# Attention with pairs of heads on the two halves of the matmul array, results feature-major

## The chip, the cores and the metric

One core of one Trainium2 chip. The time is device microseconds of one execution; a kernel's time is the median of its runs, and lower is better. PE is the matmul engine, PEld its weight loads, DVE the vector engine, ACT the scalar engine, POOL the general engine, SP the engine that issues most DMAs.

## The reference

256 tokens with 1024 features pass through two stacked blocks of two layers each, all in float32. The attention of the first block has 8 heads of 64 features in three dilation groups, whose results are mixed by a softmax over their log-sum-exps; the kernel takes that as one softmax over the keys of all three groups. The second block has 8 query heads on 2 key heads, with a learned sink in the denominator, beside a Fourier mix; both halves are normed and projected.

```
# first block, per layer
x = x + 0.5 * swiglu_ffn(rmsnorm(x, ffn1_norm), ffn1_w_up, ffn1_w_down)
q, k, v, glu_in, gates = split(rmsnorm(x, mix_norm) @ w_in + b_in)
q, k = apply_rope(rmsnorm(q, q_norm)), apply_rope(rmsnorm(k, k_norm))
for g, (window, dil) in enumerate(((128, 1), (512, 4), (2048, 16))):
    o, l = dilated_window_attn(q[:, :, g], k[:, :, g], v[:, :, g], dil, window // (2 * dil))
y_attn = sum(softmax(lses)[..., None] * outs) @ w_attn_proj
y_conv = conv_module(glu_in, ...)
x = x + (sigmoid(g_attn) * y_attn + sigmoid(g_conv) * y_conv) @ w_out
x = rmsnorm(x + 0.5 * swiglu_ffn(rmsnorm(x, ffn2_norm), ...), final_norm)

# second block, per layer
u, q, k, v = split(rmsnorm(x, norm1) @ w_in)
y_f = real(fft2(u, norm="ortho")) @ w_f + b_f
s = where(|qpos - kpos| <= 128, (q . k) / 8, -inf)      # 4 query heads share one key head
y_a = softmax(concat(s, sink))[..., :-1] @ v
x = x + concat(rmsnorm(y_f, g_fourier_out), rmsnorm(y_a, g_attn_out)) @ w_o
x = x + (silu(conv3(h @ w_gate)) * conv3(h @ w_val)) @ w_down    # h = rmsnorm(x, norm2)
```

## The kernel before, in words

The residual stream lives on chip with features on partitions: eight tiles of [128 features, 256 tokens]. Every weight passes through on-chip memory once, in units of at most [128, 1024], in the order of use. `unit` (L317) hands out the next one; `ahead` (L304) splits it into a rounded part on ACT (L312) and the rest on DVE (L313), three units ahead, and `fetch` (L294) loads six ahead on SP's queue. A float32 product of weights is three passes of a faster float32r format on such split operands: `mm3` (L326 to L332). Products in the attention are plain float32, which PE runs as two instructions each.

The program is written in one order; a scheduler in the compiler then orders each engine's instructions by that priority and by when it reckons them ready, so that neighbouring pieces can interleave. Two pools hold the accumulators, four banks each of [128, 512]: `acc` (for products of weights) and `aux` (scores, transposes, sums).

First block, `mixer` (L620). q and k are normed, rotated and transposed to features on partitions, two heads to a tile of 128 rows (64 rows each); v stays with tokens on partitions. Attention goes over 16 steps a layer, (tile of 128 queries, head), in a pipeline of three (L816 to L839): `scores` (L765) of step i, one product of 256 keys and two of 128 keys on the 64 rows of the head; `soft` (L774), mask and maximum on DVE (L777), exp with its sum on ACT (L779); `pv_transpose` (L886) of step i-1, four transposes (L889) of the unnormalised probabilities and a copy (L891); `pv` (L782) of step i-2, four products with the transposed probabilities standing and 64 columns of v streaming (L785), result with tokens on partitions. Half units of the gates' products (`gate`, L806, 24 instructions) stand between the steps. `finish` (L789), once per tile of queries, divides by the sums (L793) and transposes the result to features on partitions (L797) for the projection. The mean and variance of the conv branch (`norm_mean`, `norm_cols`, `norm_rows`) run at steps 2, 5 and 7.

Second block, `mixer2` (L899). Eight steps a layer (L1108 to L1122), each for two heads of one parity, which lie on the same 64 rows: `soft` (L1064) with two scores of 256 keys (L1069), mask (L1074), exp (L1080); then transposes and `pv` (L1084, products L1088). The Fourier products (`f1`, `f2`, `f3`) and the first half of the projection (`proj(0, .)`) fill in by the table `fill` (L1046). `finish` (L1090) divides, takes the mean square of the result over its features on ACT and scales by its inverse root; `attn_operand` (L1123) transposes the result (L1127) and splits it. `proj(1, ob)` (L1024) adds the attention half to x.

The two edges of a half-array product in the code of before:

```
pr, ro = h // 2, slice((h % 2) * HD, (h % 2) * HD + HD)
nc.tensor.matmul(s[:, :256], qT[0][ro, pr, ts], kT[0][ro, pr, :], start=True, stop=True)
nc.tensor.matmul(Y[t][:, h * HD:(h + 1) * HD], pT[:, i * P:(i + 1) * P], w, start=i == 0, stop=i == 3)
```

Of the kernel before, what the change touches and what calls it, by code (L numbers as in the profile page):

```python
"""Two stacked transformer blocks (dilated-attention conformer, then a Fourier / windowed-GQA block),
256 tokens, 1024 features, two layers each, on one core.

The residual stream lives on chip feature-major: eight tiles [128 features, 256 tokens].
Every weight passes through SBUF once, in the order of its use.  Each float32 product is three
float32r passes on operands that are split on chip into a rounded part and the rest:
W x = Wl xh + Wh xl + Wh xh.
In the first block the tokens are ordered by (t mod 4, t div 4), so that the dilated groups are
blocks on the diagonal of a tile of 128 queries.
"""  # L10
# [45 lines left out]
FIRST = {1: -5, 3: -4, 5: -3, 7: -2}  # L56
# buffers of the weight stream, and how many units its splits and its loads run ahead
# [70 lines left out]
def shape_tables():  # L128
# [29 lines left out]
    # cosines at the frequencies 0..128, sines at 1..127: the rest follows by symmetry  # L158
# [35 lines left out]
# ----------------------------------------------------------------------------------------------  # L194
class Kernel:
# [130 lines left out]
    def mm3(self, out, wh, wl, xh, xl, start, stop, skip=False):  # L326
        """out += W^T x, stationary W"""
# [6 lines left out]
    def split(self, src, hi, lo, scale=None):  # L334
        """hi = rounded src * scale, lo = the rest"""
# [10 lines left out]
    def behind(self):  # L346
        """The block's work on ScalarE and VectorE queues up behind the last split."""
# [4 lines left out]
    def square_sum(self, blocks, scales=None):  # L352
        """Sum over blocks of (block * scale)^2, elementwise on [128, 256]"""
# [951 lines left out]
```

## Time and profile before

| | |
|---|---|
| median of 3 runs | 2011.82 us (1998.09, 2011.82, 2012.04) |
| profiled execution, its span | 1994.0 us |
| PE busy | 1972.2 us, 99% |
| DVE busy | 1393.5 us, 70% |
| ACT busy | 1121.9 us, 56% |
| attention stages, first block | 374 to 456 and 1066 to 1150 us |
| attention stages, second block | 1454 to 1504 and 1736 to 1787 us |

The profiled execution's own time beside its span is not recorded apart from the three runs; the fastest of them, 1998.09 us, is 4.1 us above its span. Times in the profile count from the first instruction. Durations of PE's instructions include their way through the array and overlap; the distance between two starts is what one costs in a stream.

### The profile page before, as it was taken

What the parts mean: (1) busy time and instruction counts of PE and PEld (TensorE: products, weight loads), DVE (VectorE), ACT (ScalarE), POOL (GpSimd) and SP (SyncE); (2) the same over time, 40 slices, a digit from 0 to 9 for tenths busy, and PEclk for the clock granted to TensorE, in tenths of its full rate; (3) what the DMA queues carried; (4) which work ended last, traced back from release to release, by engine and by line L of the source; (5) the groups of instructions that cost most, each with busy time, mean ns of one, the idle gap of its engine ahead of it and who ended that gap; (6) DMA issues with size and microseconds to landing.
All of it is one profiled execution on the core that took longest, in us unless ns stands there. A gap on an engine that the chain in (4) does not pass through costs nothing. (4 is left out here: it accounts for less than half of the span.)

```text
span 1994.0 us, 37071 instructions
## 1 busy us (share of the span) xinstructions
PE 1972.2 (99%) x14760; PEld 1881.0 (94%) x14760; DVE 1393.5 (70%) x2364; ACT 1121.9 (56%) x2133; POOL 113.9 (6%) x111
## 2 busy tenths in 40 slices
PE   8999999999999999999999999999999999999999
PEld 8999878899999999998788999999889999899999
DVE  6765687857666576656877567666768985669973
ACT  5544555647544455445556575444676764577662
POOL 1000022100000000000212000000100000100000
PEclk9999999999999999999999999999999999999999
DMA  8655655434555555556545245556334655524654
GB/s 263 194 179 182 218 169 167 154 96 159 180 182 183 176 177 191 175 185 212 177 165 165 79 154 180 183 178 182 122 127 149 199 177 179 181 96 161 203 179 125
DMA packets 97260, 339.09 MB, mean 170 GB/s; under 512 B 11430, under 2 KB 13574, under 8 KB 96960
## 3 DMA queue, kind: packets, MB, share of 16 engines
q1 hardware_dynamic: 93024, 326.63, 50.5%
q0 software_dynamic: 2944, 8.11, 1.7%
q8 instruction: 115, 1.88, 0.4%
q10 hardware_dynamic: 1120, 2.00, 0.3%
q14 instruction: 57, 0.47, 0.1%
HBM read 335.65 MB, written 1.05 MB: 169 GB/s over the span
## 5 line engine op out<-in xcount | busy, mean ns | idle before, releaser
L313 DVE TENSOR_TENSOR wl<-raw,wh 128x1024 fp32r<-128x1024 f32 (+1 forms) x634 | 758.7, 1199 | 351.2 <-ACT wh L312 346.2
L312 ACT ACTIVATE wh<-raw 128x1024 fp32r<-128x1024 f32 (+1 forms) x634 | 655.3, 1037 | 582.8 <-PE acc L332 273.1
L330 PE MATMUL acc<-xh,wl 128*128 128x256 f32 x1760 | 502.8, 286 | 4.6 <-DVE wl L313 4.5
L331 PE MATMUL acc<-xh,wh 128*128 128x256 f32 x1760 | 499.7, 284 | 0.0
L332 PE MATMUL acc<-xl,wh 128*128 128x256 f32 x1760 | 498.5, 283 | 0.0
L330 PEld LDWEIGHTS acc<-xh,wl 128*128 128x128 f32 x1760 | 338.1, 192 | 6.3 <-DVE wl L313 5.3
L331 PEld LDWEIGHTS acc<-xh,wh 128*128 128x128 f32 x1760 | 338.2, 192 | 0.8
L332 PEld LDWEIGHTS acc<-xl,wh 128*128 128x128 f32 x1760 | 338.0, 192 | 0.0
L330 PE MATMUL acc<-hh,wl 128*128 128x256 f32 x1056 | 298.8, 283 | 0.0
L331 PE MATMUL acc<-hh,wh 128*128 128x256 f32 x1056 | 298.8, 283 | 0.0
L332 PE MATMUL acc<-hl,wh 128*128 128x256 f32 x1056 | 298.8, 283 | 0.0
L330 PEld LDWEIGHTS acc<-hh,wl 128*128 128x128 f32 x1056 | 202.8, 192 | 0.0
L331 PEld LDWEIGHTS acc<-hh,wh 128*128 128x128 f32 x1056 | 202.8, 192 | 0.0
L332 PEld LDWEIGHTS acc<-hl,wh 128*128 128x128 f32 x1056 | 202.8, 192 | 0.0
L578 PE MATMUL acc<-wl,xh 128*128 128x512 f32 x480 | 189.7, 395 | 0.5 <-DVE wl L313 0.5
L579 PE MATMUL acc<-wh,xh 128*128 128x512 f32 x480 | 187.9, 392 | 0.0
L580 PE MATMUL acc<-wh,xl 128*128 128x512 f32 x480 | 187.8, 392 | 0.0
L330 PE MATMUL acc<-xn,wl 128*128 128x256 f32 x608 | 172.1, 283 | 0.0
L331 PE MATMUL acc<-xn,wh 128*128 128x256 f32 x608 | 172.1, 283 | 0.0
L332 PE MATMUL acc<-xn,wh 128*128 128x256 f32 x608 | 172.1, 283 | 0.0
L330 PEld LDWEIGHTS acc<-xn,wl 128*128 128x128 f32 x608 | 116.7, 192 | 0.0
L331 PEld LDWEIGHTS acc<-xn,wh 128*128 128x128 f32 x608 | 116.7, 192 | 0.0
(278 smaller groups left out, 3072.3 us busy)
## 6 DMA issues: line engine op xcount, KB each, us to landing
raw<-wts SPq DMA_DIRECT2D x576, 512.0 KB, 3.4
raw<-wts SPq DMA_DIRECT2D x48, 384.0 KB, 3.1
brow<-b_in POOLq DMA_DIRECT2D x26, 256.0 KB, 3.8
raw<-dft SPq DMA_DIRECT2D x4, 512.0 KB, 3.5
tab<-tab ACTq DMA_DIRECT2D x1, 1024.0 KB, 8.1
out<-x SPq DMA_DIRECT2D x8, 128.0 KB, 3.5
raw<-dft SPq DMA_DIRECT2D x2, 384.0 KB, 3.4
wraw<-conv_w POOLq DMA_DIRECT2D x6, 124.0 KB, 4.9
```

What stands on the lines that cost most here:

```text
L312: nc.scalar.activation(h[:, :n], r[:, :n], AF.Copy)
L313: nc.vector.tensor_tensor(lo[:, :n], r[:, :n], h[:, :n].bitcast(F32), op=ALU.subtract)
L330: mm(out, wl, xh, start=start, stop=False, **k)
L331: mm(out, wh, xh, start=False, stop=False, **k)
L332: mm(out, wh, xl, start=False, stop=stop, **k)
L578: mm(accs[t], xh[k][:, ts], wl[:, c], start=k == 0, stop=False)
L579: mm(accs[t], xh[k][:, ts], wh[:, c], start=False, stop=False)
L580: mm(accs[t], xl[k][:, ts], wh[:, c], start=False, stop=k == KB - 1)
```

## The change

In both blocks a step takes two heads whose features lie on the two halves of the 128 rows. First block: 8 steps a layer, (pair of heads, tile of queries); the scores of the two heads alternate, each into its own `aux` bank. The probabilities are divided by their sum before the transposes. In `pv`, 64 columns of v stand and the transposed probabilities stream; the two heads' results go to the lower and upper 64 partitions of one bank, so the result has features on partitions, and `finish` only splits it. The results take two `acc` banks from the start of the attention. One or two half gates stand in each of ten iterations. Second block: 4 steps a layer, (key head, tile of queries), each with four heads, two on each half; `fill` is regrouped to six iterations of three pieces. The inverse root of the attention output's mean square is taken by a sum over partitions and applied to the product of `proj(1, .)`. Comments and docstrings are removed throughout, with the line numbers kept; those hunks are left out, and of removed lines (they stand above) only the first of a run.

```diff
@@ -758,47 +758,50 @@
             if j + 2 < len(QKV):
                 rows.append(bias_row(QKV[j + 2][0] * AW + QKV[j + 2][1] * 512))
         self.exp_table()
-        Y = [None, None]
...
+        half = lambda h: slice(h * HD, (h + 1) * HD)
+        Y = [self.acc("Y") for _ in range(2)]
+        def scores(t, j):
+            s = [self.aux("s") for _ in range(2)]
             ts = slice(t * P, (t + 1) * P)
-            nc.tensor.matmul(s[:, :256], qT[0][ro, pr, ts], kT[0][ro, pr, :], start=True, stop=True)
...
+            for g in range(3):
+                c, ks = (slice(0, 256), slice(0, 256)) if g == 0 else (slice(128 + g * P, 256 + g * P), ts)
+                for h in range(2):
+                    nc.tensor.matmul(s[h][:, c], qT[g][half(h), j, ts], kT[g][half(h), j, ks], start=True, stop=True)
             return s
-        def soft(t, h, s, rden):
...
+        def soft(t, s):
+            e = [self.t2("e") for _ in range(2)]
+            m, rden = self.small("m", 2), self.small("rden", 2)
+            for h in range(2):
+                nc.vector.tensor_tensor_reduce(e[h], s[h], self.m1[t], scale=1.0, scalar=-3e38, op0=ALU.add, op1=ALU.max,
+                                               accum_out=m[:, h:h + 1])
             nc.vector.tensor_scalar_mul(m, m, -1.0)
-            stat["exp"] = nc.scalar.activation(e, e, AF.Exp, bias=m, scale=1.0, accum_out=rden[:, h:h + 1])
+            for h in range(2):
+                stat["exp"] = nc.scalar.activation(e[h], e[h], AF.Exp, bias=m[:, h:h + 1], scale=1.0,
+                                                   accum_out=rden[:, h:h + 1])
+            nc.vector.reciprocal(rden, rden)
+            for h in range(2):
+                nc.vector.tensor_scalar_mul(e[h], e[h], rden[:, h:h + 1])
             return e
-        def pv(t, h, pT):
...
+        def pv(t, j, pT):
+            ks = [(0, 0), (0, 1), (1, t), (2, t)]
+            out = Y[j // 2][:, j % 2 * S + t * P:j % 2 * S + (t + 1) * P]
+            for i, (g, tt) in enumerate(ks):
+                for h in range(2):
+                    c = tt * 512 + (j * 2 + h) * HD
+                    nc.tensor.matmul(out[half(h)], vv[g].rearrange("p a b -> p (a b)")[:, c:c + HD], pT[h][:, i * P:(i + 1) * P],
+                                     start=i == 0, stop=i == 3)
         yT = [self.t4("yTh", F32R), self.t4("yTl", F32R)]
-        def finish(t, den):
...
+        def finish(i):
+            self.split(Y[i].rearrange("p (j c) -> p j c", j=2), *[y[:, i * 2:i * 2 + 2] for y in yT])
         blk = lambda tiles, b: tiles[b // 4][:, b % 4]
         ga, gc = [self.t4("ga"), self.t4("ga")], [self.t4("gc"), self.t4("gc")]
@@ -812,32 +815,30 @@
                 nc.vector.tensor_tensor(blk(ga, n), a[:, :256], R, op=ALU.mult)
                 nc.vector.tensor_tensor(blk(gc, n), a[:, 256:], R, op=ALU.mult)
-        steps = [(t, h) for t in range(2) for h in range(NH)]
...
+        steps = [(j, t) for j in range(NH // 2) for t in range(2)]
+        later = {1: norm_mean, 3: norm_cols, 4: norm_rows}
+        gates = [(n, hf) for n in range(KB) for hf in range(2)]
         soft1, tr1 = None, None
         for i in range(len(steps) + 2):
             soft0 = tr0 = None
             if i < len(steps):
-                t, h = steps[i]
-                soft0 = (t, h, soft(t, h, scores(t, h), den[t]))
+                j, t = steps[i]
+                soft0 = (j, t, soft(t, scores(t, j)))
+            gate(*gates.pop(0))
             if soft1 is not None:
-                tr0 = (soft1[0], soft1[1], self.pv_transpose(soft1[2]))
-            if i % 4 != 3:
+                tr0 = (*soft1[:2], [self.pv_transpose(e) for e in soft1[2]])
+            if i % 2 == 0:
                 gate(*gates.pop(0))
             if tr1 is not None:
-                t, h, pT = tr1
...
+                j, t, pT = tr1
+                pv(t, j, pT)
+                if j % 2 and t:
+                    finish(j // 2)
             if i in later:
                 later[i]()
             soft1, tr1 = soft0, tr0
         def sigmoids(g, o_):
             with self.tc.issue_after(stat["silu"].ins):
                 for i in range(KB):
@@ -1032,7 +1033,9 @@
                 kk = half * 4 + k
                 self.mm3(out, wh[:, c], wl[:, c], oph[kk], opl[kk], k == 0 and ob % 2 == 0, k == 3, skip=True)
             if half == 1:
-                nc.vector.tensor_tensor(x[ob], x[ob], out, op=ALU.add)
+                t = self.t1("as")
+                nc.vector.tensor_tensor(t, out, cell["Ra"], op=ALU.mult)
+                nc.vector.tensor_tensor(x[ob], x[ob], t, op=ALU.add)
         def fourier_sum(ob):
             t = self.t1("fs")
@@ -1043,95 +1046,90 @@
         def later(name, f):
             return lambda: cell.update({name: f()})
-        fill = {0: [lambda: f1(0)], 1: [lambda: f1(1)], 2: [lambda: f2(0)], 3: [lambda: f2(1)],
...
+        fill = {0: [lambda: f1(0)], 1: [lambda: f1(1), lambda: f2(0)], 2: [lambda: f2(1), lambda: (f3(0), f3(1))],
+                3: [lambda: (f3(2), f3(3)), later("s", lambda: self.square_sum([yf[:, b] for b in range(4)]))],
+                4: [lambda: proj(0, 0), lambda: proj(0, 1), later("c", lambda: self.rms_cols(cell["s"], 512))],
+                5: [lambda: proj(0, 2), lambda: proj(0, 3), later("R", lambda: self.rows(cell["c"]))]}
         def piece(i, j):
-            if i in fill and j < len(fill[i]) and fill[i][j] is not None:
+            if i in fill and j < len(fill[i]):
                 fill[i][j]()
-        heads = lambda pr: ((pr // 2) * 4 + pr % 2, (pr // 2) * 4 + pr % 2 + 2)
...
+        half = lambda h: slice(h * HD, (h + 1) * HD)
+        Y = [self.acc("Y") for _ in range(2)]
+        heads = lambda kv, h: slice(kv * 4 + h, kv * 4 + h + 3, 2)
+        def soft(t, kv):
             ts = slice(t * P, (t + 1) * P)
-            s = self.aux("s")
...
+            s = [self.aux("s") for _ in range(2)]
             for j in range(2):
-                c = slice(j * 256, (j + 1) * 256)
...
+                for h in range(2):
+                    mm(s[h][:, j * 256:(j + 1) * 256], qT[half(h), kv * 2 + j, ts], kT[half(h), kv, :], start=True, stop=True)
+            e = [self.t2("e") for _ in range(2)]
+            mx, nm, den, se = [self.small(n, 4) for n in ("mx", "nm", "den", "se")]
+            for h in range(2):
+                for j in range(2):
+                    c = slice(j * 256, (j + 1) * 256)
+                    nc.vector.tensor_tensor_reduce(e[h][:, c], s[h][:, c], self.m2[t], scale=1.0, scalar=-3e38, op0=ALU.add,
+                                                   op1=ALU.max, accum_out=mx[:, h * 2 + j:h * 2 + j + 1])
+            for h in range(2):
+                hs = slice(h * 2, h * 2 + 2)
+                nc.vector.scalar_tensor_tensor(nm[:, hs], mx[:, hs], -1.0, nsink[:, heads(kv, h)], op0=ALU.mult, op1=ALU.min)
+                nc.vector.tensor_tensor(se[:, hs], sink[:, heads(kv, h)], nm[:, hs], op=ALU.add)
+            nc.scalar.activation(se, se, AF.Exp)
+            for h in range(2):
+                for j in range(2):
+                    c, i = slice(j * 256, (j + 1) * 256), h * 2 + j
+                    nc.scalar.activation(e[h][:, c], e[h][:, c], AF.Exp, bias=nm[:, i:i + 1], scale=1.0,
+                                         accum_out=den[:, i:i + 1])
+            nc.vector.tensor_tensor(den, den, se, op=ALU.add)
+            nc.vector.reciprocal(den, den)
+            for h in range(2):
+                for j in range(2):
+                    c, i = slice(j * 256, (j + 1) * 256), h * 2 + j
+                    nc.vector.tensor_scalar_mul(e[h][:, c], e[h][:, c], den[:, i:i + 1])
             return e
-        def pv(t, pr, pT):
...
+        def pv(t, kv, pT):
+            out = Y[kv].rearrange("p (j c) -> p j c", j=2)[:, :, t * P:(t + 1) * P]
+            for i in range(2):
+                w = vt[:, i * P + kv * HD:i * P + (kv + 1) * HD]
+                for h in range(2):
+                    mm(out[half(h)], w, pT[h].rearrange("p (j i c) -> p j i c", j=2, i=2)[:, :, i], start=i == 0, stop=i == 1,
+                       skip_group_check=True)
+        def finish(kv):
+            y = ya[:, kv * 2:kv * 2 + 2]
+            nc.scalar.activation(y, Y[kv].rearrange("p (j c) -> p j c", j=2), AF.Copy)
+            for j in range(2):
+                i = kv * 2 + j
+                self.split(ya[:, i], oph[4 + i], opl[4 + i], self.v(l, "g_attn_out_2", i))
+        ya = self.t4("ya")
+        steps = [(kv, t) for kv in range(2) for t in range(2)]
         soft1 = tr1 = None
         for i in range(len(steps) + 2):
-            soft0 = (*steps[i], soft(*steps[i])) if i < len(steps) else None
+            soft0 = (*steps[i], soft(steps[i][1], steps[i][0])) if i < len(steps) else None
             piece(i, 0)
-            tr0 = (*soft1[:2], self.pv_transpose(soft1[2])) if soft1 is not None else None
+            tr0 = (*soft1[:2], [self.pv_transpose(e) for e in soft1[2]]) if soft1 is not None else None
             piece(i, 1)
             if tr1 is not None:
-                t, pr, pT = tr1
...
+                kv, t, pT = tr1
+                pv(t, kv, pT)
+                if t:
+                    finish(kv)
+            piece(i, 2)
             soft1, tr1 = soft0, tr0
-        def attn_operand():
...
+        later("sa", lambda: self.square_sum([ya[:, b] for b in range(4)]))()
         for ob in range(4, KB):
-            if ob == KB - 1:
-                attn_operand()
             proj(0, ob)
             fourier_sum(ob - 4)
+            if ob == 5:
+                later("ca", lambda: self.rms_cols(cell["sa"], 512))()
+        later("Ra", lambda: self.rows(cell["ca"]))()
         for ob in range(4, KB):
             fourier_sum(ob)
```

## Rows read from the trace of the kernel before

**Rows 1.** The page's first part: busy time, share of the span and instructions of an engine.

```profile
PE 1972.2 (99%) x14760; PEld 1881.0 (94%) x14760; DVE 1393.5 (70%) x2364; ACT 1121.9 (56%) x2133; POOL 113.9 (6%) x111
```

**Rows 2.** PE's waits over the whole span: total us, times, longest us.

```profile
PE acc L330 <- DVE wl L313: 4.5, 2, 3.6
PE tr L562 <- DVE z L550: 3.7, 4, 1.1
```

**Rows 3.** Windows, the four attention stages: length, busy us of each engine, granted clock, DMA.

```profile
374.00:456.00 82.00, 81.85 (x632) 76.89 (x631) 46.91 (x109) 43.58 (x79) 1.83 (x3) 1.00 0.34 109
1066.00:1150.00 84.00, 82.75 (x605) 76.16 (x604) 52.40 (x116) 46.47 (x104) 5.72 (x4) 1.00 0.34 108
1454.00:1504.00 50.00, 49.82 (x351) 44.27 (x352) 31.82 (x97) 33.49 (x85) 2.36 (x4) 0.93 0.31 102
1736.00:1787.00 51.00, 50.19 (x371) 44.69 (x371) 35.07 (x99) 35.97 (x92) 1.81 (x3) 1.00 0.33 111
```

**Rows 4.** Groups by line and shape, whole span: busy us, mean ns, idle before.

```profile
L785 PE MATMUL Y<-qkv,pT 128*128 128x64 f32 x256 | 32.1, 268 | 0.0
...
L769 PE MATMUL s<-qkv,qkv 64*128 64x256 f32 x64 | 22.3, 428 | 0.0
```

**Rows 5.** PE's timeline, one step of the first block: start us, us, instruction.

```profile
383.37 0.28 PE L332 MATMUL acc<-xl,wh 128*128 128x256 f32 x1
383.57 0.70 PE L769 MATMUL s<-qkv,qkv 64*128 64x256 f32 x2
384.11 0.60 PE L771 MATMUL s<-qkv,qkv 64*128 64x128 f32 x4
384.64 0.66 PE L889 MATMUL pt<-ident,e 128*128 128x128 f32 x4
385.06 0.36 PE L330 MATMUL acc<-xh,wl 128*128 128x256 f32 x1
385.26 0.28 PE L331 MATMUL acc<-xh,wh 128*128 128x256 f32 x1
...
388.01 1.00 PE L785 MATMUL Y<-qkv,pT 128*128 128x64 f32 x8
388.85 0.43 PE L372 MATMUL sum<-cs,ones 128*128 128x256 f32 x1
```

**Rows 6.** PE's timeline, one step of the second block.

```profile
1478.81 1.00 PE L1088 MATMUL Y<-v,pT 128*128 128x64 f32 x8
1479.74 1.13 PE L1069 MATMUL s<-kT,qT 64*128 64x256 f32 x4
1480.80 0.39 PE L330 MATMUL acc<-yfh,wl 128*128 128x256 f32 x1
```

**Rows 7.** Groups of DVE and ACT by line and shape, whole span.

```profile
L1080 ACT ACTIVATE e<-e,nm 128x256 f32<-128x256 f32 x32 | 15.9, 497 | 5.5 <-DVE nm L1077 5.4
...
L383 DVE TENSOR_SCALAR diag<-ident,rc 128x128 f32<-128x128 f32 x28 | 8.0, 373 | 8.8 <-POOL rc L404 8.8
...
L793 DVE TENSOR_TENSOR y<-Y,rd 128x512 f32<-128x512 f32 x4 | 2.8, 692 | 0.3
```

**Rows 8.** Windows inside the first and the third stage.

```profile
374.00:414.00 40.00, 39.85 (x300) 36.71 (x299) 27.48 (x67) 20.55 (x41) 0.70 (x1) 1.00 0.40 131
1454.00:1464.00 10.00, 9.89 (x42) 7.76 (x42) 4.41 (x14) 5.45 (x12) 0.00 (x0) 0.66 0.41 146
```

**Rows 9.** PE's timeline at the head of the third stage, idle and releaser in brackets.

```profile
1452.77 0.50 PE L970 MATMUL acc<-wh,uh 128*128 128x256 f32 x2 [1.00 <-ACT uh L341]
1454.11 0.39 PE L971 MATMUL acc<-wh,ul 128*128 128x256 f32 x1 [0.84 <-DVE ul L342]
```

More of the change, by code (lines that the diff above doesn't have):

```diff
@@ L762, in mixer @@
         self.exp_table()
-        Y = [None, None]
-        def scores(t, h):
-            pr, ro = h // 2, slice((h % 2) * HD, (h % 2) * HD + HD)
-            s = self.aux("s")
+        half = lambda h: slice(h * HD, (h + 1) * HD)
+        Y = [self.acc("Y") for _ in range(2)]
+        def scores(t, j):
+            s = [self.aux("s") for _ in range(2)]
             ts = slice(t * P, (t + 1) * P)
-            nc.tensor.matmul(s[:, :256], qT[0][ro, pr, ts], kT[0][ro, pr, :], start=True, stop=True)
-            for g in (1, 2):
-                nc.tensor.matmul(s[:, 128 + g * P:256 + g * P], qT[g][ro, pr, ts], kT[g][ro, pr, ts], start=True, stop=True)
-            return s
@@ L774, in soft @@
-        def soft(t, h, s, rden):
-            e = self.t2("e")
-            m = self.small("m", 1)
-            nc.vector.tensor_tensor_reduce(e, s, self.m1[t], scale=1.0, scalar=-3e38, op0=ALU.add, op1=ALU.max, accum_out=m)
-            nc.vector.tensor_scalar_mul(m, m, -1.0)
-            stat["exp"] = nc.scalar.activation(e, e, AF.Exp, bias=m, scale=1.0, accum_out=rden[:, h:h + 1])
-            return e
-        def pv(t, h, pT):
-            vt = lambda g, tt: vv[g].rearrange("p a b -> p (a b)")[:, tt * 512 + h * HD:tt * 512 + (h + 1) * HD]
-            for i, w in enumerate((vt(0, 0), vt(0, 1), vt(1, t), vt(2, t))):
-                nc.tensor.matmul(Y[t][:, h * HD:(h + 1) * HD], pT[:, i * P:(i + 1) * P], w, start=i == 0, stop=i == 3)
@@ L813, in gate @@
                 nc.vector.tensor_tensor(blk(gc, n), a[:, 256:], R, op=ALU.mult)
-        steps = [(t, h) for t in range(2) for h in range(NH)]
-        den = [self.small("den", 8) for _ in range(2)]
-        later = {2: norm_mean, 5: norm_cols, 7: norm_rows}
-        gates = [(n, half) for n in range(KB) for half in range(2)]
+        steps = [(j, t) for j in range(NH // 2) for t in range(2)]
+        later = {1: norm_mean, 3: norm_cols, 4: norm_rows}
+        gates = [(n, hf) for n in range(KB) for hf in range(2)]
         soft1, tr1 = None, None
@@ L1084, in pv @@
-        def pv(t, pr, pT):
-            for j, h in enumerate(heads(pr)):
-                for i in range(2):
-                    w = vt[:, i * P + (h // 4) * HD:i * P + (h // 4 + 1) * HD]
-                    mm(Y[t][:, h * HD:(h + 1) * HD], pT[:, (2 * j + i) * P:(2 * j + i + 1) * P], w, start=i == 0, stop=i == 1)
-        def finish(t):
-            se = self.small("se", 8)
-            nc.vector.tensor_tensor(se, sink, nmx[t], op=ALU.add)
-            nc.scalar.activation(se, se, AF.Exp)
-            nc.vector.tensor_tensor(den[t], den[t], se, op=ALU.add)
-            rd = self.small("rd", 8)
-            nc.vector.reciprocal(rd, den[t])
-            y = self.t2("y")
-            nc.vector.tensor_tensor(y.rearrange("p (h d) -> p h d", d=HD), Y[t].rearrange("p (h d) -> p h d", d=HD),
-                                    rd[:, :, None].to_broadcast([P, NH, HD]), op=ALU.mult)
-            sq = self.t2("ysq")
-            sa = self.small("sa", 1)
-            nc.scalar.activation(sq, y, AF.Square, accum_out=sa)
-            nc.vector.tensor_scalar(sa, sa, 1.0 / 512, EPS, op0=ALU.mult, op1=ALU.add)
-            ra = self.rsqrt_small(sa, 1)
-            nc.scalar.activation(y, y, AF.Copy, scale=ra)
-            yn[t] = y
@@ L1108, in mixer2 @@
-        steps = [(t, pr) for t in range(2) for pr in range(4)]
+        half = lambda h: slice(h * HD, (h + 1) * HD)
+        Y = [self.acc("Y") for _ in range(2)]
+        heads = lambda kv, h: slice(kv * 4 + h, kv * 4 + h + 3, 2)
+        def soft(t, kv):
+            ts = slice(t * P, (t + 1) * P)
+            s = [self.aux("s") for _ in range(2)]
+            for j in range(2):
+                for h in range(2):
[23 more added lines that the diff above has]
+                    nc.vector.tensor_scalar_mul(e[h][:, c], e[h][:, c], den[:, i:i + 1])
+            return e
@@ L1114, in mixer2 @@
             piece(i, 1)
             if tr1 is not None:
-                t, pr, pT = tr1
-                if pr == 0:
-                    Y[t] = self.aux("Y")
-                pv(t, pr, pT)
-                if pr == 3:
-                    finish(t)
-            soft1, tr1 = soft0, tr0
-        def attn_operand():
-            for i in range(4):
-                p = self.aux("ytr")
-                for t in range(2):
-                    nc.tensor.transpose(p[:, t * P:(t + 1) * P], yn[t][:, i * P:(i + 1) * P], self.ident)
-                self.split(p[:, :256], oph[4 + i], opl[4 + i], self.v(l, "g_attn_out_2", i))
+                kv, t, pT = tr1
```

41 lines of the change are left out of this document (removed).

## Prediction

> **What bounds the kernel now.** I read the engine totals first: the matmul engine PE is busy 1972.2 of 1994.0 us, DVE 1393.5, ACT 1121.9 [rows 1]. A busy PE could still be a waiting one, so the list of PE's waits came next: its two longest lines are 4.5 and 3.7 us over the whole run [rows 2]. So PE's own queue sets the end, and an edit is worth what it takes out of that queue, less the waits it puts in. The change touches four stretches, the attention of two layers in each block. In all four PE is busy to within 1.3 us (81.85 of 82, 82.75 of 84, 49.82 of 50, 50.19 of 51), while DVE has 46.9 of 82 and 31.8 of 50, ACT 43.6 of 82 and 33.5 of 50 [rows 3]. Together they are 267 us, so only part of some 13% of the span is at stake.
>
> Mean durations overlap (268 ns for a 64-column product, 428 for a 256-column score [rows 4]), so I price PE by the distance between starts, from the timeline of one step. A float32 product is two instructions.
>
> **What the steps cost before.** First block, one head of 128 queries [rows 5]: two score instructions of 256 columns take 383.57 to 384.11, four of 128 columns 384.11 to 384.64. Four transposes take 0.42, so 0.105 to 0.11 per 128 streamed columns, and 256 columns of float32 0.21. Pure streaming of the scores is then 2 x 0.213 + 4 x 0.11 = 0.87, but from the end of the last gate product (383.37 + 0.12) to the first transpose it is 1.15, and the second gate product after the transposes comes 0.20 after the first instead of 0.12: going into the 64-row products and out again costs about 0.35. Eight value products take 388.01 to 388.85, 0.105 each, though they stream only 64 columns: the 128-column weight load sets their pace. Second block, two heads [rows 6]: eight value products 0.93 with the step into the scores, four scores 1.06, of which 0.85 is streaming; in and out is about 0.40.
>
> Per layer before:
> first block: scores 16 x (0.87 + 0.35) = 19.5; values 16 x 0.84 = 13.4; eight transposes of the result (two at the end of each tile of four) 8 x 0.11 = 0.9; sum 33.8 us.
> Second block: 8 x (0.85 + 0.40) = 10.0; 8 x 0.84 = 6.7; eight transposes 1.0; sum 17.7 us.
>
> **The change, part by part.** The transposes of the probabilities (16 or 8 times four a layer), the gates and the Fourier products stay as many as they were: nothing.
>
> Scores. Their number stays; the two heads of a pair alternate, one on the lower and one on the upper 64 rows, each into its own bank, and the 16 entries into that mode become 8 (8 become 4). What no row shows is whether products on the two halves run side by side. Bounds: one after the other, 8 x (1.74 + 0.35) = 16.7 in the first block and 4 x (1.71 + 0.40) = 8.4 in the second; fully side by side, 8 x (0.87 + 0.1 + 0.35) = 10.6 and 4 x (0.85 + 0.2 + 0.4) = 5.8 (0.1 and 0.2 for the ends of the staggered pair). I take a middle for the first block: if streams share but loads don't, twelve loads at the 0.105 of the value products give 1.26, so 8 x (1.26 + 0.1 + 0.35) = 13.7. With 256 columns two loads fit under one stream, so 5.8 stays.
>
> Values. Now v stands (64 columns wide) and the probabilities stream 128 (first block) or 256 columns (second), twice as many columns per head, on two column halves. One after the other: 16 x 0.11 = 1.76 per pair; and as column halves are a new mode, I charge the 0.35 to 0.40 that the score rows show: 8 x 2.11 = 16.9 and 4 x (1.71 + 0.4) = 8.4, dearer than before. Side by side: 8 x (0.88 + 0.1 + 0.35) = 10.6 and 4 x 1.45 = 5.8. I take side by side, because the score rows already show a half-array mode in use at full streaming rate; both ends stay in the range.
>
> The result's transposes go (0.9 and 1.0). The second block's norm of the attention output moves behind the projection: four one-column products and four 128-column ones are added, 8 x 0.1 = 0.8 a layer.
>
> PE per layer after: 13.7 + 10.6 = 24.3 (saves 9.5) and 5.8 + 5.8 + 0.8 = 12.4 (saves 5.3); two layers each, 29.6 us. One after the other everywhere: 0.2 and 0.1, so 0.6 us: nothing. With loads shared as well: 12.6 + 5.3, so 35.8.
>
> The Trainium skill, TensorE: Matmul & The Clock Gate, section "Part 3: Packing small matmuls", says that a weight load overlaps running products only when its row group differs. Both value halves use all rows, so by it every slot would hold a load and a stream, some 0.05 + 0.11 instead of 0.11, and the sum would lose about 9 of the 29.6 us. The trace differs: the value products of [rows 5] start every 0.105, the time of the load alone, so their stream hides on the same rows; I keep the larger sum.
>
> **Vector and scalar work.** The division by the sum moves from the result to the probabilities: in the first block 16 products of [128, 512] a layer, priced between 0.373 (a [128, 128] product with a column) and 0.692 (the [128, 512] one that goes) [rows 7]. At 0.69 they are 11.0 us a layer, less 2 x 0.69. The first 40 us of that stage have DVE busy 27.5 [rows 8], with the conv's mean in them; half the addition makes 33 in some 35, nearly full. In the second block 16 products of [128, 256], about 0.42, add 6 to 7 us to 31.8 in a stretch of some 45, and eight more after the projection 3.4, with x of the feed forward queued behind them on DVE. PE's queue hides these while it has other products to issue.
>
> Where the cover is thin is the head of a stage. The pair's softmax must finish before its transposes, and it now has four masks, four exps (0.497 each [rows 7]), a reciprocal and two products where there were two masks and two exps: about 3.5 us later in the second block. Behind it on ACT stands the split that the next Fourier product waits for. The results also hold two of four accumulator banks throughout, so fewer products can run ahead. Waits added: at least 0 (all of PE's waits before were short), at most about 3.5 x 4 = 14 us; I take 7. Net saving 29.6 - 7 = 22.6 us.
>
> **Against the run's own time.** The profiled span is 1994.0 and the fastest run 1998.1, some 4 us around it; that execution would come to about 1975. The median, 2011.8, is 13.7 above the fastest run, which the trace doesn't explain; taking the saving from the median gives 1989 us, and I leave room for the lower level.
>
> **Rivals.** About 1% (20 us) is what a measurement of this kernel tells from no change.
> (a) The halves don't run side by side. For it: no row shows two products at once. Against: half-array products already stream at full rate. Saving 0.6, waits of about 4: 2015 us. Then the change doesn't do what it says.
> (b) Rows share, columns don't: first block 5.8 + 0.9 - 3.5, second 4.2 - 1.7 + 0.2, twice, 11.8; less 7: 2007 us.
> (c) Slower: PE runs dry at the head of each stage and its clock falls. At 1454 us PE waited 1.00 and 0.84 us, and the ten microseconds around have a mean granted clock of 0.66, between the 1.2 and the 2.4 GHz level, a loss of some 3.4 us [rows 8, 9]. Four stages at 3.5 + 3.4 are 27.6 us: 2039 if nothing is shared, still about no change if it is. It decides only where the sharing saves less than some 7 us.
> (d) Loads share too: 35.8 - 7, 1983 us.
>
> The Trainium skill, TensorEngine Tiling (Array Packing), section "Key Properties", says that tiles work in parallel, loads included, and that changing the mode drains the engine; by the first half (d) would be the case. The gaps around the scores in [rows 5] agree with the second half; nothing in this trace shows the first.
>
> **How the numbers follow.** Forecast 0.58, (a) 0.17, (b) 0.11, (c) 0.08, (d) 0.06. The likeliest is 1989 us; its own range is 1975 to 2000. To hold eight in ten, I reach up to (a) and down to the fastest run less 32: 1966 to 2015. Faster by over 1%: two thirds of the forecast and nearly all of (d), 0.45. Slower: (c), 0.08. Within 1%: the rest, 0.47.
>
> **What would show it.** Right: the scores of a pair in about 1.7 us in the first block and 1.45 in the second, instructions of the two halves starting in couples; the sixteen value products of a pair within about 0.9 us instead of 1.76; the stages shorter by about 8 us in the first block and 3.5 in the second, after waits. Wrong: starts at 0.11 and 0.21 throughout (a); PE waits on the products of DVE or on the transposes of over 14 us in sum, or a granted clock under 1 at the heads of the stages (c); DVE full in the first stage with PE waiting on it.

## The result and the profile after

The changed kernel takes 1981.2 us (median of 4 runs, 1979.1 to 1982.5); the kernel before 2005.0 (4 runs, 1994.1 to 2012.0, three of them those of the table ahead). The ratio is 0.989, with a 95% interval of 0.9851 to 0.9929: faster by 24 us, about 1%. Four runs with a spread of 18 us make that figure a loose one: against the 31 runs of the kernel before that stand beside experiments 1 to 4 (median 2001.4) it would be 20. The forecast was 1989 (1966 to 2015), a net saving of 22.6. The profiled execution has a span of 1979.4 us against 1994.0, so it shows 14.6 us only; the missing 9 us lie in the spread of the kernel before, which goes with its clock, as told under experiment 3.

The totals answer to [rows 1]: PE does 25 us less, DVE 26 more, and PE is still by far the busiest engine.

```profile
span 1979.4 us, 36996 instructions
PE 1947.0 (98%) x14680; PEld 1847.7 (93%) x14680; DVE 1419.1 (72%) x2460; ACT 1115.5 (56%) x2139; POOL 111.2 (6%) x109
```

First, did the halves run side by side? PE's groups by line of the kernel after; the figure behind the bar is the busy time of the group, overlaps counted once. They answer to [rows 4].

```profile
L798 PE MATMUL Y<-pT,qkv 128*64 128x128 f32 x256 | 17.5, 279 | 0.0
L773 PE MATMUL s<-qkv,qkv 64*128 64x256 f32 x64 | 14.0, 446 | 2.3 <-ACT pT L892 2.3
L1068 PE MATMUL s<-kT,qT 64*128 64x256 f32 x64 | 12.2, 484 | 0.0
L773 PE MATMUL s<-qkv,qkv 64*128 64x128 f32 x128 | 12.1, 282 | 0.0
L1100 PE MATMUL Y<-pT,v 128*64 128x256 f32 x64 | 10.8, 417 | 0.0
```

The three such groups of the kernel before that were not shown ahead:

```profile
L771 PE MATMUL s<-qkv,qkv 64*128 64x128 f32 x128 | 19.9, 273 | 0.0
L1069 PE MATMUL s<-kT,qT 64*128 64x256 f32 x64 | 19.7, 426 | 0.0
L1088 PE MATMUL Y<-v,pT 128*128 128x64 f32 x128 | 16.2, 269 | 0.0
```

The mean of one score in the first block is nearly what it was (446 against 428 ns, 282 against 273), as many of them run, and yet the groups are busy 38.3 us instead of 61.9. The values fall from 48.3 to 28.3. So two products are on the array at once. PE's timeline of one step of the first block (the answer to [rows 5]) gives the price of a pair of heads:

```profile
396.32 0.28 PE L332 MATMUL acc<-xl,wh 128*128 128x256 f32 x1
396.53 1.09 PE L798 MATMUL Y<-pT,qkv 128*64 128x128 f32 x16
397.55 1.15 PE L773 MATMUL s<-qkv,qkv 64*128 64x256 f32 x12
398.63 0.39 PE L330 MATMUL acc<-xh,wl 128*128 128x256 f32 x1
```

From start to start, sixteen value products take 1.02 us and twelve scores 1.08, the way in and out included. Inside such a group the starts come in couples some 6 ns apart, loads as well as products.

Next, what became of it: windows by stage (length, busy us of each engine, granted clock). In order: the first block's attention in layers 0 and 1; the second block's token products, its attention and the feed forward's pairs in layer 0; its attention in layer 1. These stretches run to the end of each stage and are longer than those of [rows 3].

```profile
374.00:449.90 75.90, 74.44 (x684) 69.58 (x684) 57.91 (x135) 49.38 (x96) 1.83 (x3) 1.00 0.40 132
1062.40:1142.80 80.40, 77.02 (x683) 71.25 (x683) 59.25 (x137) 49.41 (x96) 0.72 (x1) 0.96 0.35 119
1391.70:1433.90 42.20, 36.26 (x178) 29.59 (x176) 33.47 (x69) 29.53 (x79) 9.91 (x7) 0.90 0.38 126
1433.90:1517.00 83.10, 81.21 (x579) 72.28 (x578) 62.91 (x176) 51.31 (x120) 2.22 (x3) 0.89 0.36 118
1517.00:1628.10 111.10, 110.37 (x913) 109.74 (x913) 102.64 (x193) 77.88 (x130) 0.00 (x0) 1.00 0.54 178
...
1723.00:1801.50 78.50, 75.85 (x580) 68.80 (x579) 63.38 (x176) 51.46 (x121) 2.13 (x3) 0.96 0.40 129
```

The same stages of the kernel before, cut at the same instructions:

```profile
374.30:463.40 89.10, 88.95 (x691) 84.13 (x691) 52.86 (x123) 50.18 (x93) 1.83 (x3) 1.00 0.34 111
1076.10:1165.20 89.10, 88.97 (x692) 84.17 (x692) 53.05 (x125) 50.22 (x93) 1.24 (x2) 1.00 0.33 105
1414.00:1454.80 40.80, 35.81 (x177) 29.40 (x175) 32.91 (x66) 29.55 (x79) 9.46 (x6) 0.92 0.38 120
1454.80:1535.50 80.70, 80.63 (x611) 75.21 (x611) 57.71 (x149) 52.62 (x120) 3.99 (x5) 0.96 0.39 127
1535.50:1645.00 109.50, 109.50 (x915) 109.50 (x914) 101.05 (x187) 77.03 (x126) 0.00 (x0) 1.00 0.55 181
...
1739.70:1817.80 78.10, 77.87 (x611) 73.05 (x611) 57.37 (x147) 52.61 (x121) 3.45 (x4) 1.00 0.39 130
```

The first block gains 13.2 and 8.7 us, where the prediction looked for about 8. The second block, where it looked for 3.5 a layer, gains nothing: its attention is 2.4 and 0.4 us longer, the token products ahead of it 1.4 in layer 0, and the pairs behind it 1.6 in each layer (layer 1: 111.1 against 109.5). PE, which was idle 0.1 to 0.2 us in each attention stage, is now idle 1.5, 3.4, 1.9 and 2.7, and in three of them its mean clock is under 1. Its waits name the places; they answer to [rows 2]:

```profile
PE sumc L397 <- DVE sacc L365: 4.3, 5, 2.0
...
PE sum L372 <- DVE m L780: 2.6, 1, 2.6
PE s L773 <- ACT pT L892: 2.3, 2, 1.5
PE pt L890 <- DVE e L1091: 2.2, 2, 1.1
PE acc L332 <- DVE xn L339: 1.4, 4, 0.5
```

### The profile page after: what moved, and what is told of

Same layout as the page of the kernel before. It is cut to its first block, busy times and chain, and to the rows that moved or that the text cites. A ratio compares the mean times of both kernels' runs of the same rounds, so it can differ in the third digit from the quotient of the medians.

```text
span 1979.4 us, 36996 instructions
## 1 busy us (share of the span) xinstructions
PE 1947.0 (98%) x14680; PEld 1847.7 (93%) x14680; DVE 1419.1 (72%) x2460; ACT 1115.5 (56%) x2139; POOL 111.2 (6%) x109
```

## The experiments

All times are medians, of ten runs in experiments 1 to 4, of two in 11 and of four in the others; the interval is that of the ratio to the runs of the kernel before that were made beside them. These were 1 to 4, 5 to 8, 9 to 11 and 12 together, with medians of the kernel before of 2001.4, 2000.8, 1998.7 and 1996.6, so a few us between experiments of different sets can't be told.

**1. Scores one half after the other** (both blocks; the second block's loops likewise).

```diff
-            for g in range(3):
-                c, ks = (slice(0, 256), slice(0, 256)) if g == 0 else (slice(128 + g * P, 256 + g * P), ts)
-                for h in range(2):
+            for h in range(2):
+                for g in range(3):
+                    c, ks = (slice(0, 256), slice(0, 256)) if g == 0 else (slice(128 + g * P, 256 + g * P), ts)
```

> The changed kernel with the scores of a pair issued head after head (all products of the lower half, then all of the upper half), in both blocks; same products, nothing else. Theory (the halves run side by side, loads too: twelve instructions in 0.88 us in the first block, eight in 0.85 in the second): a pair's scores go to about 1.6 to 1.7 us in both blocks, PE gets some 0.75 us longer per pair, 24 pairs-and-tiles in all, so 15 to 20 us slower than the changed kernel's 1981 (less what fills waits at the heads of the stages), about 1997. Rival (the gain is only fewer mode changes, the couples in the trace are an artefact of the records): within 3 us of 1981.

1991.4 us, ratio 0.9952 (0.9926 to 0.9979): 10 slower than the change. The direction is the theory's, the size is not.

**2. Values one half after the other** (the loop over h put outside that over the key blocks, both blocks):

> The changed kernel with the value products of a pair issued head after head, in both blocks; same products, nothing else. Theory (column halves run side by side: sixteen instructions in 0.82 us): a pair's value products go to 1.6 to 1.75 us, some 0.85 us more for 24 pairs-and-tiles, 17 to 21 us slower than the changed kernel, about 2000. Rival (columns share no better in turns than one after the other): within 3 us of 1981.

1988.5 us, 0.9929 (0.9901 to 0.9957): 7 slower. The timelines say why so little. PE, scores apart, then values apart:

```profile
408.96 1.68 PE L773 MATMUL s<-qkv,qkv 64*128 64x256 f32 x12
410.57 0.39 PE L330 MATMUL acc<-xh,wl 128*128 128x256 f32 x1
```

```profile
422.27 1.58 PE L798 MATMUL Y<-pT,qkv 128*64 128x128 f32 x16
423.79 1.15 PE L773 MATMUL s<-qkv,qkv 64*128 64x256 f32 x12
```

A pair of scores takes 1.61 instead of 1.08, not the 2.09 that I had priced for no sharing; values 1.52 instead of 1.02, not 2.11. Eight pairs in two layers make 14 x 0.53 + 2 x 0.10 = 7.6 for the scores (the first pair of a layer goes to 1.18 only) and 16 x 0.50 = 8.0 us for the values. In the second block two of a layer's four pairs are issued in two groups of four score instructions; each group goes from 0.63, at full clock, to 1.06 (8 x 0.43 = 3.4), and the values stayed at 1.02. The sums, 11.0 and 8.0, are near the measured 10 and 7. The rest of the sharing survived because PE does not keep to the program's order between halves, as told in the last section: these edits undid half of it. The theory that side by side is the saving holds; its full size these two runs bound from below only.

**3. First block alone, 4. second block alone** (the other block's functions as before):

> The first block's attention as changed, the second block's as before. Theory (first block saves 13.3 and 8.7 us in the two profiles, the second block gives back about 7 through PE waiting at the head of its stages, the clock falling there, and the longer work on DVE after the projection): faster than the changed kernel by 5 to 8 us, about 1975. Rival (the second block's loss is chance in where the clock fell, its saved products are worth the 5 us a layer of PE's queue): slower than the changed kernel by up to 10 us.

> The first block's attention as before, the second block's as changed. Theory: PE's saved time there is spent waiting, so not faster than before; 0 to 8 us slower than the runs of before that lie beside it. Rival: 5 to 10 us faster than before.

The second block alone: 2003.0 us, 1.0013 (0.9991 to 1.0036): worth nothing, as expected. Its attention stage of layer 1:

```profile
1741.80:1819.90 78.10, 72.88 (x580) 65.81 (x580) 64.17 (x178) 51.93 (x121) 2.14 (x3) 1.00 0.41 131
```

PE is busy 72.9 us at full clock where it was busy 77.9: 5.0 saved, and 5.2 idle in place of 0.2. The pairs behind it take 111.1 us, as in the change.

The first block alone: 1981.1 us, 0.9905 (0.9871 to 0.9938), not the 1975 expected: ten runs from 1967.9 to 1988.0. Its profile, with a span of 1986.1 us, has a bad stretch in the old second block:

```profile
1432.00:1442.00 10.00, 8.48 (x30) 6.33 (x31) 6.25 (x15) 6.29 (x15) 0.00 (x0) 0.66 0.64 196
1442.00:1452.00 10.00, 10.00 (x41) 8.04 (x41) 1.53 (x6) 3.05 (x10) 0.00 (x0) 0.50 0.00 0
1452.00:1462.00 10.00, 10.00 (x47) 9.05 (x47) 4.92 (x13) 4.67 (x14) 0.00 (x0) 0.50 0.33 107
1462.00:1472.00 10.00, 10.00 (x53) 8.98 (x51) 3.73 (x12) 5.09 (x17) 0.00 (x0) 0.63 0.16 53
```

PE waits (on the splits of u ahead of the first Fourier product), its clock goes to the 1.2 GHz level and stays there for some 30 us in which PE is full. This attention stage took 93.0 us; in the profile of before, where the clock came back after some 10 us [rows 8], it took 80.7. Across the 52 runs of the kernel before in these sessions the time follows the run's mean granted clock (correlation -0.98): 1992.0 at 0.998, 2001.4 at 0.992, 2012.3 at 0.986. A spread of this kind is the likely source of the 13.7 us between the median and the fastest run that the prediction could not explain; the clocks of those three runs are not on record.

**5, 6. Other orders of the second block's pieces.**

The lambdas and the last two slots are left out here; f1 first (5), and f3 later as well (6):

```diff
-        fill = {0: [f1(0)], 1: [f1(1), f2(0)], 2: [f2(1), (f3(0), f3(1))],
-                3: [(f3(2), f3(3)), s],
+        fill = {0: [f1(0), f1(1)], 1: [f2(0)], 2: [f2(1), (f3(0), f3(1))],
+                3: [(f3(2), f3(3)), s],
```

```diff
+        fill = {0: [f1(0), f1(1)], 1: [f2(0)], 2: [f2(1)],
+                3: [(f3(0), f3(1)), (f3(2), f3(3)), s],
```

> The change, with one piece moved: in the second block the second half of the first Fourier product (f1(1)) is issued in the first step, before the second pair's scores, and the first f2 has the slot before the first transposes. Theory: the heads of the second block's attention lose time because the split of f1's result stands on ACT behind eight exps and because only f1 covers the first pair's softmax; with this order the waits of the first transposes on the division (2.2 us in all) and of f2 on the split go, the clock after the head falls less, and the run takes 1975 to 1978 us, 3 to 6 below the change's 1981. Rival: the clock falls because of the waits on the split of u ahead of f1, which stay; then the waits go but the time is within 2 us of 1981.

> As the kernel with f1 first, and the four f3 pieces one slot later, behind the first pair's values and the third and fourth pair's scores, so that two stretches of PE work lie between the second f2 and f3, which waits for the split of f2's result. In the kernel with only the second block changed, PE waited 3.5 us on that split on ACT and 1.7 on its DVE part, in two layers. Theory (the second block's attention gains 5 us a layer in PE's work and gives it back in waits at pieces that are too close to what they wait for): 1971 to 1976 us. Rival (ACT and DVE are simply full in the first 30 us, the order does not matter): within 2 us of the kernel with f1 first.

1982.5 (0.9856 to 0.9935) and 1981.2 us (0.9845 to 0.9939): no gain; my theory of the pieces' order fell. The wait of the transposes on the division, which was to go, is 2.2 us in both as in the change, and others grew. In the kernel with f3 later the wait on the split that it was to remove is among the longest of all:

```profile
PE acc L330 <- ACT yfh L338: 5.0, 2, 2.5
...
PE pt L890 <- DVE e L1092: 2.2, 2, 1.1
```

**7. Banks of the first block.** The bank of a result is taken at its first values, and the conv's norm sums use the products' pool:

```diff
-        Y = [self.acc("Y") for _ in range(2)]
+        Y = []
...
+                if j % 2 == 0 and t == 0:
+                    Y.append(self.acc("Y"))
...
-        p = self.aux("sum")
+        p = self.one("sum")
```

(likewise sumc and rows; one() gives a bank of acc while the norm's pieces run.)

> The change, with the accumulator banks of the first block's attention dealt out otherwise: the bank for a pair of pairs' results is taken when its first values are issued instead of at the start, and the sums of the conv's norm (sum, sumc, rows) take a bank of the products' pool instead of one of the four that scores and transposes share. Theory: the waits of the sum on the mask (2.6 us, layer 1) and of the scores on the copies of the transposes (2.3 us, two times) are a lack of banks, and the fall of the clock in layer 1 follows from them: both go, layer 1's stage takes 76 to 77.5 us instead of 80.4, the run 1975 to 1978. Rival: DVE and ACT are late whatever bank is free, the wait moves to the next product: layer 1's stage stays above 79.5 and the run is within 2 us of 1981.

1975.8 us, 0.986 (0.9821 to 0.99): 5.4 faster than the change; the time and the stage are the theory's. The two waits that it named are gone from the list of PE's waits, and one of the scores on the mask, in layer 1, has come:

```profile
PE s L776 <- DVE m L783: 2.2, 1, 2.2
```

The first block's stages:

```profile
374.90:448.50 73.60, 73.60 (x684) 69.06 (x684) 57.22 (x134) 47.97 (x94) 1.82 (x3) 1.00 0.42 135
1062.50:1139.10 76.60, 74.39 (x684) 69.41 (x684) 58.21 (x136) 47.96 (x94) 0.72 (x1) 1.00 0.38 123
```

PE is never idle in layer 0; in layer 1 it is idle 2.2 us instead of 3.4, and its clock stays at full speed. The edit eases both pools at once, so it doesn't tell which of its two moves was needed. This also gives the saving of PE itself: 89.1 - 73.6 = 15.5 us a layer.

**8. Both (6 and 7)**:

> Both of the above: the second block's pieces as in the kernel with f3 later, and the first block's banks as in the kernel with banks dealt out otherwise. If both theories hold the gains add, since the stages lie 300 us apart: 1966 to 1972 us, 9 to 15 below the change. If either rival holds, the time is that of the better of the two alone.

1975.0 us, 0.9857 (0.9818 to 0.9896): that of 7 alone. Against 6, which differs from it by the banks alone, it is 6.3 faster, and their runs don't overlap (1974.3 to 1976.1, 1978.9 to 1983.8): the banks' worth a second time.

**9. First block as in 7, second block as before.**

> The first block as in the kernel with its banks dealt out otherwise, the second block as in the kernel before. Theory (the change's part in the second block is worth nothing at full clock, since what it takes from PE comes back as waits and in the eight multiplies behind the projection): the first block's stages of 73.6 and 76.5 instead of 89.1 each give 28 us, the feed forward's pairs take 109.4 again; the best runs near 1964, the median 1968 to 1976 with a spread of over 10 us, since the old second block brings its fall of the clock (93 instead of 81 us in one layer) in some runs. Rival (the second block's side by side products pay): no run below 1972 and a median above 1980.

1974.8 us, 0.9869 (0.982 to 0.9917), from 1966.5 to 1981.2. Against 7 (1973.5 to 1977.9) the medians agree: as far as four runs tell, the second block's part of the change is worth nothing in the median, and what it does is to narrow the spread. Experiment 4 has the same: ten runs from 1999.5 to 2005.3, where 31 of the kernel before go from 1992.0 to 2013.0.

**10. The second block's softmax half by half** (on top of 7: exp of the sink, sum, reciprocal and division in one loop over h):

> The kernel with the first block's banks dealt out otherwise, and in the second block's softmax the sums, the reciprocal and the division done half by half, so that the first half's transposes wait for two exps instead of four. Theory: the waits in the second block come from the long chain of a pair's softmax (four masks, four exps, sum, reciprocal, four divisions one behind the other on two engines that are idle a quarter of that time): the waits of the transposes on the division go from 2.2 us to under 1, the second block's idle time falls by 1 to 3 us a layer, 1970 to 1974 us. Rival: ACT and DVE hand over as often and the next wait takes the place, within 2 us of 1975.8.

1972.8 us, 0.9861 (0.9816 to 0.9906). The wait that was aimed at shrank, others did not, and a new one of the values came:

```profile
PE acc L334 <- ACT yfh L342: 3.0, 2, 1.5
...
PE pt L897 <- DVE e L1100: 1.3, 2, 0.6
PE Y L1109 <- DVE den L1096: 1.3, 2, 0.6
```

The second block's idle time in the two attention stages (79.70 - 75.98 and 78.40 - 74.35, so 7.8) is not below that of 7 (7.3). The 3 us by which the median lies lower can't be told from the spread; this one is inconclusive.

**11. Without the scalings.**

> The change without the divisions of the probabilities in both blocks and without the eight multiplies by the attention's 1/rms behind the second block's projection (these parts of the computation are left out; the chains that yield the divisors stay). The three lie in stretches of their own. Theory: DVE's work that was to be hidden is hidden only in part. First block: 7.7 us less on DVE a layer, layer 0 from 75.8 to 74 or less, layer 1 from 80.4 to 77 or less; second block: the attention of layer 1 from 78.5 to 76 or less; the feed forward's pairs from 111.1 to 109.4. Rival (the divisions are covered, banks and the order of ACT set the waits): the attention stretches within 0.5 us of the change's at the same clock, and only the pairs shorter.

1974.1 us, of two runs. First block's layer 0, then the second block's attention of layer 0, that of layer 1 and the pairs behind it:

```profile
374.90:451.90 77.00, 75.58 (x684) 70.71 (x683) 51.88 (x119) 49.01 (x96) 1.83 (x3) 0.98 0.39 129
...
1437.10:1516.30 79.20, 75.73 (x579) 69.14 (x579) 57.75 (x159) 52.66 (x123) 2.22 (x3) 0.95 0.37 124
...
1720.60:1798.40 77.80, 76.82 (x580) 70.05 (x580) 58.23 (x159) 52.72 (x124) 2.14 (x3) 0.93 0.40 132
1798.40:1907.80 109.40, 109.40 (x914) 109.40 (x914) 100.15 (x177) 77.12 (x126) 0.00 (x0) 1.00 0.53 181
```

In the first block the rival is right, the division was covered: without it the stages are no shorter (77.0 us at clock 0.98, as in experiment 3 with the division, and 80.7 in layer 1 against 80.4). In the second block the division was not wholly covered, but its size is not settled. The second block exactly as in the change ran three times: in the change, in 4 and in 7. Its layer 0 took 83.1, 81.0 and 80.5 us there, its layer 1 78.5, 78.1 and 78.6, with PE idle from 2.5 to 5.2 us in layer 1 as its clock went from 0.96 to 1.00: a slower PE waits less, so neither the idle time nor length times clock can be compared alone. Without the division the stages take 79.2 and 77.8, shorter than each of them, by 1.3 to 3.9 and 0.3 to 0.8 us. The eight multiplies cost the pairs their 1.6.

**12. The attention's 1/rms onto the result's four blocks**, one column block of the projection earlier, on top of 10:

> The kernel with the softmax half by half, and the attention's 1/rms multiplied onto the four blocks of the result ahead of their splits, one projection column block earlier, instead of onto the eight blocks behind the projection. Theory: the eight multiplies on DVE stand ahead of the feed forward's operands and cost 1.7 us a layer there (111.1 against 109.4, as the kernel without scaling showed); four multiplies beside the last two column blocks of the Fourier half's projection are covered: the pairs take 109.4, the run 1968 to 1971 us. Rival: the chain from the last values over the sum, the reciprocal root and the row to the four splits is longer than the 5.2 us of those two column blocks, PE waits 2 to 4 us ahead of the attention half's projection and what is won is lost: 1972 to 1976.

1973.4 us, 0.9868 (0.98 to 0.9936). The pairs are back at 109.5 (row below), and the attention ahead of them is 0.4 and 0.3 us longer than in 10, so the time should have fallen, but the median is the rival's:

```profile
1512.30:1621.80 109.50, 109.50 (x915) 109.50 (x914) 100.81 (x186) 76.98 (x126) 0.00 (x0) 1.00 0.54 181
```

In this run the token products of layer 0 took 44.3 us at a mean clock of 0.89 (42.4 at 0.91 in 10). So 7, 8, 9, 10 and 12 all have medians below both kernels and lie within 3 us of each other; which is best is open.

## Why the prediction was right

The time is in the range and the sign is right; the net saving was 22.6 forecast, 24 measured between the medians and 14.6 between the profiles. That the number came so near is luck in good part: it is the difference of two terms, and both were too small, the saving on PE by 11 us and what comes back by 19.

- **PE's queue is the bound**: held for the kernel before, whose PE idles 0.1 to 0.2 us in each of these stages.
- **Side by side**: held, rivals (a) and (b) are out. The term that failed is the scores of the first block, "if streams share but loads don't", 13.7 us a layer. Loads are shared: 8 x 1.08 = 8.6. The values, 10.6 forecast, took 8 x 1.02 = 8.2, since the way in and out of a group costs 0.2 and not 0.35. With both, PE saves 15.5 us a layer (experiment 7) where 9.5 stood. In the second block 5.0 (experiment 4) where 5.3 stood. That is 41.0 in place of 29.6. The prediction's own 33.8 less these 8.6 and 8.2 would be 17.0 and not 15.5, because its price of before was too dear too: summed from start to start over the whole stage of before, the scores take 17.5 (19.5 forecast), the values 14.0 (13.4) and the transposes 0.9. Rival (d), with a chance of 0.06, had the mechanism, and its 1983 is the nearest of the stated times.
- The Trainium skill, TensorEngine Tiling (Array Packing), "Key Properties", says that tiles load and multiply in parallel: the 1.08 us agree. The Trainium skill, TensorE: Matmul & The Clock Gate, "Part 3: Packing small matmuls", lets a load overlap running products only where the row group differs; the sixteen value products, all on 128 rows, take 1.02 us with their loads among them, so this trace differs, as that of before had hinted.
- **Division**: 0.69 a multiply was too dear. DVE's groups after have 0.48 and 0.35:

```profile
L788 DVE TENSOR_SCALAR e<-e,rden 128x512 f32<-128x512 f32 x32 | 14.1, 482 | 0.3
L1091 DVE TENSOR_SCALAR e<-e,den 128x256 f32<-128x256 f32 x32 | 9.1, 349 | 0.2
```

  "PE's queue hides these" is true of the first block; in the second, the eight multiplies behind the projection cost 1.6 us a layer, and the division something that is not settled (experiment 11).
- **Waits, taken as 7, range 0 to 14**: the other failed term. In the profiled run 41.0 became 14.6, so 26 came back. From the windows: the first block 31.0 - 21.9 = 9.1 (idle 4.8; the clock of layer 1, by an estimate 0.04 x 80.4 = 3.2); the second block's attention 10.0 + 2.8 = 12.8 (idle 4.5, the division among its causes; the rest clock, 0.11 x 83.1 = 9.1 in layer 0 against 0.04 x 80.7 = 3.2 before, and 0.04 x 78.5 = 3.1 in layer 1 against nothing); the pairs 3.2; the token products 1.5. So about 12 us are falls of the clock, which the sum had at nothing and only rival (c) priced; layer 0 of the second block was a bad one in that run (the same code took 80.5 in 7). Of the first block's wait I had probably named the wrong pool: both waits that went in experiment 7 were for banks of the four that scores, transposes and the norm's sums share, and not of the products' four, but 7 eased both pools. That easing them shortens the wait and lifts the clock of layer 1 (from 0.96 to 1.00 in 7, to 0.98 in 10 and 12) is shown by these runs; in the second block it is shown that order alone does not help (5, 6), that the eight multiplies are the pairs' loss (11, 12) and that the attention is shorter without the division, by 0.3 to 3.9 us a layer (11); which of the remaining handovers between ACT, DVE and PE costs most stays open.
- **Rival (c)**, a falling clock at the heads: the mechanism is real, and one sign that the prediction gave for it, a clock under 1 there, came. This is PE at the head of the second block in the changed kernel, ten microseconds a row:

```profile
1432.00:1442.00 10.00, 8.24 (x51) 6.55 (x51) 7.34 (x32) 5.07 (x16) 0.00 (x0) 0.83 0.36 120
1442.00:1452.00 10.00, 9.93 (x47) 7.91 (x48) 5.34 (x22) 4.77 (x15) 0.00 (x0) 0.53 0.01 2
1452.00:1462.00 10.00, 10.00 (x47) 7.79 (x47) 6.85 (x21) 6.45 (x20) 0.00 (x0) 0.61 0.47 159
```

  It does not turn the sign, because the sharing saves more than it costs and the kernel before has falls of its own that cost up to 20 us in a run. The changed kernel's runs lie at 0.989 to 0.994, those of before at 0.986 to 0.999; the profile of before, at 0.996, is among its quicker runs. Hence 14.6 between the two profiles and 24 between the medians.

## What to carry to other kernels

Price side by side half-array work as one half's work, loads included, and, at shapes like these, 0.2 us for each change of group; then ask at once which engine now has less time for the same work, because a saving on a full PE comes back as waits wherever the chain between two of its products was only just covered. Count the banks of every pool at the moment of most use: here the banks cost 5 us of a 24 us gain, and borrowing one from the other pool and taking the results' banks later got it back. Before a median is compared with a profile, look at the granted clock of each run: here a spread almost as large as the effect goes with it.

## What the runs showed of the hardware that was not expected

Half-array float32 products overlap with nothing lost: sixteen value products start within 0.82 us, the time of eight (0.109 apart where one half runs alone, in experiment 2).

PE starts products of the other half ahead of program order. With scores apart (experiment 1) the program has all six instructions of the lower half first, in 14 of the first block's 16 pairs also as the compiler ordered it; in the trace of such a pair the first 256-column one of the upper half starts at 419.591 us, 6 ns behind the third of the lower half (419.585) and ahead of that half's last three (419.694, 419.806, 419.918). With values apart, in the second block, where each half has four instructions, all eight run in couples 13 ns apart, as if they alternated. In the first pair of each layer of experiment 1 the compiler had put the upper half's first product behind the lower half's second, so behind four instructions, and there too the couples begin at once. In all these cases the other half's first instruction started ahead of three that stand before it: in these traces runs of up to four instructions of one half need no interleaving, and longer ones do. The Trainium skill, TensorE: Matmul & The Clock Gate, "Part 3: Packing small matmuls", has the products start strictly in program order; this trace differs.
